# Splitting two casts differently: the first rows of a feed-forward weight cast last, and one low part of a projection weight made by VectorE

## The chip, the core and the metric

One core of a Trainium2 chip runs the whole kernel. The metric is the time of one execution on the device, in microseconds (us). Engines are named as in the profile: PE is TensorE's matmul (PEld its weight load), DVE is VectorE, ACT is ScalarE, POOL is GpSimd, SP is SyncE, which here only issues DMAs.

## What is computed

One transformer-like block on 512 tokens of width 1024, all in float32:

```
parts = split(x @ w_in)                      # att q,k,v; index q,k,w; mlstm q,k,v,i,f,o; two gates
q_a, k_a, q_i, k_i = rope(...)               # cos/sin of position * inv_freq, 32 angles a token
y_a = dsa_attention(q_a, k_a, v, q_i, k_i, w_i)   # index scores, top 128 keys, softmax over those
y_b = sigmoid(o) * head_norm(mlstm(...))
merged = sigmoid(gate_a) * (y_a @ w_up_a) + sigmoid(gate_b) * (y_b @ w_up_b)
h  = layer_norm(alpha * x + merged @ w_out)
ff = square(relu(h @ w_ff1)) @ w_ff2
r  = alpha * h + ff
r  = r + sigmoid(r @ w_ple_gate) * (p @ w_ple_proj)
out = layer_norm(r)
```

## The kernel before, in words

**Products in three parts.** Every float32 matrix is split in a high part (a cast to the type that TensorE multiplies, `hi`) and a low part (`lo = raw - hi`). A product is then three matmuls, `mm3` (L151 to L154): high by high, high by low, low by high. So each weight that arrives by DMA is cast once by ACT and subtracted once, by POOL or DVE, before TensorE can use it. `load_w` (L130) does this for the projections: a DMA on SP's queue into one of three raw buffers, the cast on ACT at L142, the subtraction at L145 in pieces, on POOL unless another engine is given.

**Order.** A scheduler places the instructions of each engine in one fixed order when the kernel is built, from a simulated timeline; `tc.issue_after` makes one instruction stand behind another. At run time each engine works through its own list in that order and waits on semaphores.

**The start.** `take` (L215) loads and splits x. `tables` (L266) issues the steps for the rotation's angles on DVE, each behind the one before; the steps are small (128x128 or 128x256), they end in the tile `rr`, and ACT makes `sind` and `cosd` from it (L276, L278). TensorE first makes the small columns `kv` (L285), then the index queries `iq` with `form_a` (L192): four loads `kk` of 256 rows of weights, two 128-row halves `k` each, for three token tiles. `rope` (L292) then rotates eight pairs of keys `k` of 64 columns (two products from PSUM at L297 and L299 and a sum at L303 whose two inputs are both in SBUF, then a copy on ACT at L305), and after them the tiles of `iq`. The next projection is `aq`, again with `form_a`; its weights are cast at L142 and subtracted on POOL at L145, and its first cast stands on ACT behind the last of the eight key copies.

**Before the feed-forward part.** `ple_projection` (L935) makes eight tiles `ppw` on TensorE, each stored by an ACT copy to `pws` (L943). Among them `h_factors` (L798) turns the last token tiles of h into factors `hc`. The feed-forward product w_ff1 follows a seven-product scheme (P1 to P7, in the order P1, P2, P3, P5, P7, P6, P4 for the first group). `w1_factor` (L911) splits the weight of each product in two halves of 128x1024: rows `0:2` and rows `2:4` of the four 128-row blocks. For P1, P3 and P5 it then adds another quarter of the weight into the raw tile with an accumulating DMA from POOL's queue (L919), which a later product uses: P5's weight is P1's raw tile after that addition. `ff1` (L980) goes through the blocks in the order 0, 1, 2, 3, so its first matmul reads the high part of rows `0:2`.

Of the kernel before, what the change touches and what calls it, by code (L numbers as in the profile page):

```python
# [53 lines left out]
def f(ap):  # L54
    return ap.bitcast(F32)
# [3 lines left out]
def block_kernel(ctx: ExitStack, tc: tile.TileContext, t, out):  # L59
# [67 lines left out]
    def raw_tile(shape, name):  # L127
        return rawpool.tile(shape, F32, tag="wr", bufs=3, name=name)

    def load_w(src, a, b, name, lo_eng=None, off=0, raw=None):  # L130

        raw = raw or raw_tile([P, a, b], name + "r")
        if isinstance(src, list):
            c = 0
            for s_ in src:
                sy.dma_start(raw[:, :, c:c + s_.shape[-1]], s_)
                c += s_.shape[-1]
        else:
            sy.dma_start(raw, src)
        hi, lo = (wpool.tile([P, 1088], F32R, tag="w" + x, bufs=3, name=name + x)[:, off:off + a * b]  # L140
                  .rearrange("p (a b) -> p a b", a=a) for x in "hl")
        se.copy(hi, raw)  # L142
        n = max(1, a // 4)
        for k in range(0, a, n):
            (lo_eng or ge).tensor_sub(lo[:, k:k + n], raw[:, k:k + n], f(hi[:, k:k + n]))  # L145
        return hi, lo

    def chunked(src):
        return src.rearrange("(k p) c -> p k c", p=P)
# [33 lines left out]
    xL = xpool.tile([P, KD, S], F32R, name="xL")  # L183


    def columns(kk, cols, name, lo_eng=None):
        rows = w_in[kk * 256:(kk + 1) * 256]
        return load_w([chunked(rows[:, c0:c0 + n]) for c0, n in cols], 2, sum(c[1] for c in cols), name + "w", lo_eng)

    passed = []  # L190

    def form_a(cols, name, lo_eng=None, first=0, bank=acc):  # L192

        width = sum(c[1] for c in cols)
        banks = {i: (aux if i == 0 else bank)(name + str(i)) for i in range(first, NT)}
        for kk in range(4):
            wh, wl = columns(kk, cols, name, lo_eng)
            for i in banks:
                for k in range(2):
                    kg = kk * 2 + k  # L200
                    mm = mm3(banks[i][:, :width], xH[:, kg, i * P:(i + 1) * P], xL[:, kg, i * P:(i + 1) * P],
                        wh[:, k, :], wl[:, k, :], kg == 0, kg == KD - 1)
            passed.append(mm)
        return banks
# [61 lines left out]
    def tables(n):  # L266

        for _ in range(n):
            with tc.issue_after(vector[-1].ins):
                vector.append(table_steps.pop(0)())  # L270

    for k in range(KD):
        take(k)
        tables({1: 2, 3: 3}.get(k, 0))
    tables(len(table_steps))
    se.activation(sind[:, :, 1, :], sin_, AF.Sin)  # L276
    ve.tensor_scalar(sind[:, :, 0, :], sind[:, :, 1, :], -1.0, None, op0=OP.mult)
    se.activation(cosd[:, :, 0, :], cos_, AF.Sin)  # L278
    ve.tensor_copy(cosd[:, :, 1, :], cosd[:, :, 0, :])
    b1 = [(misc if i else aux)("kv") for i in range(NT)]  # L280
    for k in range(KD):
        wh, wl = (w[:, k % 2] for w in kvw[k // 2][1:])
# [53 lines left out]
    sy.dma_start(cwb, t["conv"])  # L336
    cw, cb = cwb[:, 0:4], cwb[:, 4]

    b3 = form_a([(C_IQ, 512)], "iq", first=1)
    for i in range(NT):  # L340
        ve.tensor_scalar(wi[:, i, :], b1[i][:, 192:200], IDX_W, None, op0=OP.mult)
        ps = misc("kp")
# [499 lines left out]
    def queued(engine, op, *args, **kw):  # L842

        if engine in order_of:
            with tc.issue_after(order_of[engine].ins):
                order_of[engine] = getattr(engine, op)(*args, **kw)  # L846
        else:
            order_of[engine] = getattr(engine, op)(*args, **kw)

    order_of = {}  # L850
# [34 lines left out]
    def w1_rows(t, w):  # L885
        c = groups[t] * 1024 + w[1] * 512
        return w_ff1[w[0] * 512:(w[0] + 1) * 512, c:c + 512].rearrange("(k p) c -> p k c", p=P)

    def w1_load(t, w, issue=None):
# [14 lines left out]
        else:  # L904
            loads.append(sy.dma_start(tl, w1_rows(t, w)))

    W1_OF = {P1: B11, P2: B21, P3: B22, P5: B11, P7: B22, P6: B11, P4: B21}

    W1_ADD = {P1: B12, P5: B22, P3: B12}

    def w1_factor(t, n):  # L911

        tl = w1q[t, W1_OF[n]]
        hi, lo = (pools[1].tile([P, 4, 512], F32R, tag="w1" + x, bufs=2, name="w1" + x) for x in "hl")
        for k in (slice(0, 2), slice(2, 4)):
            queued(se, "copy", hi[:, k], tl[:, k])
            queued(ve, "tensor_sub", lo[:, k], tl[:, k], f(hi[:, k]))
            if n in W1_ADD:
                ge.dma_start(out=tl[:, k], in_=w1_rows(t, W1_ADD[n])[:, k], accum_op=OP.add)  # L919
        if n == P6:  # L920
            for k in (slice(0, 2), slice(2, 4)):
                queued(ve, "tensor_add", w1q[t, B21][:, k], w1q[t, B21][:, k], tl[:, k])
        return hi, lo
# [11 lines left out]
    def ple_projection(i, hh):  # L935

        ps = (aux if (hh, i) == (1, 2) else acc)("ppw")
        tok = slice(i * P, (i + 1) * P)
        projected[:] = [half_product(ps, lambda k: pTH[:, k, tok], lambda k: pTL[:, k, tok], blocks(wp[hh:hh + 1]))]
        if i == 0:  # L940
            pwss.append(gtile("pws", F32))
        pws = pwss[hh][:, i]
        stored[:] = [se.copy(pws, ps)]  # L943
        sy.dma_start(pwd[:, i, hh * 512:(hh + 1) * 512], pws)
# [11 lines left out]
    with tc.issue_after(projected[0].ins):  # L956
        h_factors(NT - 1)
    with tc.issue_after(turned[0].ins):
        for _ in range(2):
            ple_projection(*todo.pop(0))  # L960
    close_ln()
    close_hb()
    pools[0], close_fb = open_pool("fb", side="right")
# [469 lines left out]
```

## Time and profile before

| what | us |
|---|---|
| time before, median of 3 runs | 769.85 (769.58 to 770.32) |
| the profiled execution's own time | 769.99 |
| its span, first to last instruction | 768.3 |
| PE busy / DVE busy / ACT busy / POOL busy | 757.8 / 596.7 / 418.4 / 268.1 |
| TensorE's granted clock, mean over the span | 0.996 |

PE is busy in 99% of the span, so nearly every change of the time has to show as a change of PE's few gaps. All times below are us from the start of the span.

### The profile page before, as it was taken

What the parts mean: (1) busy time and instruction counts of PE and PEld (TensorE: products, weight loads), DVE (VectorE), ACT (ScalarE), POOL (GpSimd) and SP (SyncE); (2) the same over time, 40 slices, a digit from 0 to 9 for tenths busy, and PEclk for the clock granted to TensorE, in tenths of its full rate; (3) what the DMA queues carried; (4) which work ended last, traced back from release to release, by engine and by line L of the source; (5) the groups of instructions that cost most, each with busy time, mean ns of one, the idle gap of its engine ahead of it and who ended that gap; (6) DMA issues with size and microseconds to landing.
All of it is one profiled execution on the core that took longest, in us unless ns stands there. A gap on an engine that the chain in (4) does not pass through costs nothing.

```text
span 768.3 us, 11493 instructions
## 1 busy us (share of the span) xinstructions
PE 757.8 (99%) x4332; PEld 663.2 (86%) x4332; DVE 596.7 (78%) x979; ACT 418.4 (54%) x637; POOL 268.1 (35%) x332
## 2 busy tenths in 40 slices
PE   8999999999999999999999999999999999999995
PEld 8788888889988888878889999999988888888885
DVE  7949999965557987585896767576888988998558
ACT  5546466697756633532366556656565465555210
POOL 6654554444255437470232121212010101126341
PEclk9999999999999999999999999999999999999998
DMA  8443233222223112372089996937497799895202
GB/s 283 127 131 83 56 82 83 83 69 68 71 67 92 62 44 81 91 289 101 1 243 200 335 249 191 238 84 129 112 223 192 144 402 305 140 184 186 93 27 110
DMA packets 77544, 110.43 MB, mean 144 GB/s; under 512 B 3248, under 2 KB 38576, under 8 KB 76208
## 3 DMA queue, kind: packets, MB, share of 16 engines
q1 hardware_dynamic: 58992, 72.76, 28.9%
q0 software_dynamic: 13920, 27.27, 20.6%
q10 hardware_dynamic: 4576, 9.67, 3.6%
q8 instruction: 34, 0.56, 0.3%
q14 instruction: 22, 0.18, 0.1%
HBM read 101.29 MB, written 8.39 MB: 143 GB/s over the span
## 4 chain that ended last, share of the span: by engine, by line
PE 94%; DVE 3%; issue 1%; POOL 1%; DMA 1%; DVEq 0%; ACT 0%; POOLq 0%
PE pf L993 21%; PE pf L1224 20%; PE pg L152 5%; PE pg L154 5%; PE pg L153 5%; PE pu L154 2%; PE pu L152 2%; PE pu L153 2%; PE po L152 2%; PE po L154 2%; PE po L153 2%; PE ptp L480 1%; PE kv L285 1%; PE mv L154 1%; PE mv L153 1%
## 5 line engine op out<-in xcount | busy, mean ns | idle before, releaser
L846 DVE TENSOR_TENSOR w1l<-w1q,w1h 128x1024 fp32r<-128x1024 f32 x55 | 65.0, 1222 | 34.8 <-ACT w1h L846 34.4
L846 DVE TENSOR_TENSOR wl<-b,wh 128x2048 fp32r<-128x2048 f32 x28 | 64.8, 2313 | 10.4 <-ACT wh L846 10.4
L846 ACT CAST w1h<-w1q 128x1024 fp32r<-128x1024 f32 x55 | 55.3, 1048 | 23.6 <-PE pf L993 20.6
L919 POOL DMA_DIRECT2D w1q<-in_w_ff x24 | 29.2, 1254 | 111.7 <-DVE w1l L846 108.4
L145 POOL TENSOR_TENSOR wgl<-wgr,wgh 128x256 fp32r<-128x256 f32 x64 | 49.9, 813 | 47.5 <-ACT wgh L142 47.5
L1074 POOL DMA_DIRECT2D b<-in_w_ff x14 | 17.9, 1279 | 133.3 <-DVE wl L846 125.6
L1224 PE MATMUL pf<-wh,ah 128*128 128x512 f32 x216 | 58.1, 391 | 0.0
L1224 PE MATMUL pf<-wh,al 128*128 128x512 f32 x216 | 57.8, 389 | 0.0
L846 ACT CAST wh<-b 128x2048 fp32r<-128x2048 f32 x28 | 53.5, 1909 | 3.2 <-DMA b<-in_w_ff 3.2
L1224 PE MATMUL pf<-wl,ah 128*128 128x512 f32 x216 | 53.5, 390 | 0.0
L154 PE MATMUL pg<-xH,wgl 128*128 128x512 f32 x128 | 50.6, 395 | 0.0
L152 PE MATMUL pg<-xH,wgh 128*128 128x512 f32 x128 | 50.4, 394 | 0.0
L153 PE MATMUL pg<-xL,wgh 128*128 128x512 f32 x128 | 50.3, 393 | 0.0
L1224 PEld LDWEIGHTS pf<-wh,al 128*128 128x128 f32 x216 | 40.6, 188 | 8.5
L1224 PEld LDWEIGHTS pf<-wh,ah 128*128 128x128 f32 x216 | 40.3, 188 | 8.7 <-ACT wh L846 0.4
L1224 PEld LDWEIGHTS pf<-wl,ah 128*128 128x128 f32 x216 | 40.5, 188 | 8.4
L145 POOL TENSOR_TENSOR wul<-wur,wuh 128x128 fp32r<-128x128 f32 x64 | 36.6, 605 | 19.0 <-ACT wuh L142 19.0
L846 DVE TENSOR_TENSOR c<-c,pf 128x512 f32<-128x512 f32 x48 | 30.5, 683 | 10.2 <-ACT c L846 10.2
L846 ACT ACTIVATE c<-c 128x1024 f32<-128x1024 f32 x12 | 12.7, 1061 | 31.3 <-DVE c L846 31.3
L767 POOL TENSOR_TENSOR lag<-lag,mhalf 128x1 f32<-128x1 f32 x8 | 7.5, 941 | 61.1 <-DVE lag L766 61.1
L153 PEld LDWEIGHTS pg<-xL,wgh 128*128 128x128 f32 x128 | 24.1, 188 | 4.6
L152 PEld LDWEIGHTS pg<-xH,wgh 128*128 128x128 f32 x128 | 24.1, 188 | 4.5
(396 smaller groups left out, 2297.1 us busy)
## 6 DMA issues: line engine op xcount, KB each, us to landing
b<-in_w_ff POOLq DMA_DIRECT2D x14, 1024.0 KB, 9.1
w1q<-in_w_ff POOLq DMA_DIRECT2D x24, 512.0 KB, 7.6
w1q<-in_w_ff SPq DMA_DIRECT2D x9, 1024.0 KB, 7.6
wgr<-in_w_in SPq DMA_DIRECT2D x16, 512.0 KB, 3.8
b<-in_w_ff SPq DMA_DIRECT2D x8, 1024.0 KB, 7.0
wor<-in_w_out SPq DMA_DIRECT2D x8, 512.0 KB, 7.3
b<-in_w_ff ACTq DMA_DIRECT2D x4, 1024.0 KB, 8.8
wpgr<-in_w_ple_gate SPq DMA_DIRECT2D x8, 512.0 KB, 9.1
```

Source lines behind the costliest of these rows:

```text
L145: (lo_eng or ge).tensor_sub(lo[:, k:k + n], raw[:, k:k + n], f(hi[:, k:k + n]))
L152: te.matmul(ps, sh, mh, start=first, stop=False, **kw)
L153: te.matmul(ps, sh, ml, start=False, stop=False, **kw)
L154: return te.matmul(ps, sl, mh, start=False, stop=last, **kw)
L285: te.matmul(b1[i][:, :208], (xH, xL, xH)[kind][:, k, i * P:(i + 1) * P], (wh, wh, wl)[kind], start=k == 0 and kind == 0, stop=k == KD - 1 ...
L480: te.transpose(ps[:, slot * P:(slot + 1) * P], prs[slot // 2][:, slot % 2, j * P:(j + 1) * P], ident)
L767: ge.tensor_tensor(out=ag[:, 3:4], in0=ag[:, 2:3], in1=mhalf[:, 0:1], op=OP.pow))
L846: order_of[engine] = getattr(engine, op)(*args, **kw)
L919: ge.dma_start(out=tl[:, k], in_=w1_rows(t, W1_ADD[n])[:, k], accum_op=OP.add)
L993: mm = te.matmul(ps, w[:, k, b * P:(b + 1) * P], a[:, k], start=fresh, stop=w is lo and k == 3, skip_group_check=True)
L1074: return ge.dma_start(out=tl, in_=rows_of(g, w), accum_op=OP.add)
L1224: mm = te.matmul(banks[n, s], (al if kind == 1 else ah)[:, q, tok], (wl if kind == 2 else wh)[:, q], start=fresh and kind == 0 and q == 0, ...
```

## The change

Two edits, without new arithmetic.

First, `form_a` for `iq` gives the list of DVE's table steps as `low_by`. For the first load (`kk` 0) the low part of its first half (`k` 0, 128x512) is then made by DVE and put in the chain behind the table step that was last issued; the rest of the low parts stays on POOL. So that there are steps left to stand behind, `tables` is called for two steps only ahead of the `kv` matmuls, and for the rest, with the two sine activations and the two copies, after `form_a`.

Second, `w1_factor` for the first product (group 0, P1) splits rows `2:4` first and leaves rows `0:2` to a function `finish`, which is called in the last two tiles of `ple_projection`: the cast of rows `0:2` stands behind the store of the seventh tile `ppw`, and its subtraction and its accumulating DMA behind that.

```
-    def load_w(src, a, b, name, lo_eng=None, off=0, raw=None):
+    def load_w(src, a, b, name, lo_eng=None, off=0, raw=None, first=None):
...
         for k in range(0, a, n):
-            (lo_eng or ge).tensor_sub(lo[:, k:k + n], raw[:, k:k + n], f(hi[:, k:k + n]))
+            if k == 0 and first:
+                with tc.issue_after(first[-1].ins):
+                    first.append(ve.tensor_sub(lo[:, k:k + n], raw[:, k:k + n], f(hi[:, k:k + n])))
+            else:
+                (lo_eng or ge).tensor_sub(lo[:, k:k + n], raw[:, k:k + n], f(hi[:, k:k + n]))
...
-            wh, wl = columns(kk, cols, name, lo_eng)
+            wh, wl = columns(kk, cols, name, lo_eng, None if kk else low_by)
...
-    tables(len(table_steps))
-    se.activation(sind[:, :, 1, :], sin_, AF.Sin)
-    ve.tensor_scalar(sind[:, :, 0, :], sind[:, :, 1, :], -1.0, None, op0=OP.mult)
-    se.activation(cosd[:, :, 0, :], cos_, AF.Sin)
-    ve.tensor_copy(cosd[:, :, 1, :], cosd[:, :, 0, :])
+    tables(2)
...
-    b3 = form_a([(C_IQ, 512)], "iq", first=1)
+    b3 = form_a([(C_IQ, 512)], "iq", first=1, low_by=vector)
+    tables(len(table_steps))
+    se.activation(sind[:, :, 1, :], sin_, AF.Sin)
+    ve.tensor_scalar(sind[:, :, 0, :], sind[:, :, 1, :], -1.0, None, op0=OP.mult)
+    se.activation(cosd[:, :, 0, :], cos_, AF.Sin)
+    ve.tensor_copy(cosd[:, :, 1, :], cosd[:, :, 0, :])
...
-        for k in (slice(0, 2), slice(2, 4)):
+        def part(k):
             queued(se, "copy", hi[:, k], tl[:, k])
             queued(ve, "tensor_sub", lo[:, k], tl[:, k], f(hi[:, k]))
+
+        def add(k):
             if n in W1_ADD:
                 ge.dma_start(out=tl[:, k], in_=w1_rows(t, W1_ADD[n])[:, k], accum_op=OP.add)
+
+        if t == 0 and n == P1:
+
+            part(slice(2, 4))
+            add(slice(2, 4))
+
+            def finish(wait):
+                with tc.issue_after(wait.ins):
+                    order_of[se] = se.copy(hi[:, 0:2], tl[:, 0:2])
+                queued(ve, "tensor_sub", lo[:, 0:2], tl[:, 0:2], f(hi[:, 0:2]))
+                add(slice(0, 2))
+
+            late.append(finish)
+        else:
+            for k in (slice(0, 2), slice(2, 4)):
+                part(k)
+                add(k)
...
     with tc.issue_after(turned[0].ins):
-        for _ in range(2):
-            ple_projection(*todo.pop(0))
+        ple_projection(*todo.pop(0))
+        late.pop()(stored[0])
+        ple_projection(*todo.pop(0))
```

How this moves the engines' lists at three places. On DVE, among the table steps (`rr`, `kq` and `ang` are their tiles; `iqwl` is the low part of the index queries' weights, `wi` small columns taken from the `kv` banks). Before:

```order
L256 SCALAR_TENSOR_TENSOR rr<-kq,rr 128x256
L257 SCALAR_TENSOR_TENSOR rr<-kq,rr 128x256
L258 TENSOR_SCALAR rr<-rr 128x128
L259 TENSOR_SCALAR kq<-rr 128x256
L260 TENSOR_TENSOR rr<-rr,kq 128x256
L261 TENSOR_SCALAR kq<-rr 128x256
L262 TENSOR_TENSOR rr<-rr,kq 128x256
L263 TENSOR_SCALAR rr<-rr 128x256
L341 TENSOR_SCALAR wi<-kv 128x8
L277 TENSOR_SCALAR sind<-sind 128x4x32
L279 COPY cosd<-cosd 128x4x32
L341 TENSOR_SCALAR wi<-kv 128x8 x3
```

The same place on DVE in the changed kernel:

```order
L260 SCALAR_TENSOR_TENSOR rr<-kq,rr 128x256
L147 TENSOR_TENSOR iqwl<-iqwr,iqwh 128x512
L261 SCALAR_TENSOR_TENSOR rr<-kq,rr 128x256
L262 TENSOR_SCALAR rr<-rr 128x128
L263 TENSOR_SCALAR kq<-rr 128x256
L264 TENSOR_TENSOR rr<-rr,kq 128x256
L265 TENSOR_SCALAR kq<-rr 128x256
L266 TENSOR_TENSOR rr<-rr,kq 128x256
L267 TENSOR_SCALAR rr<-rr 128x256
L346 TENSOR_SCALAR wi<-kv 128x8 x4
L342 TENSOR_SCALAR sind<-sind 128x4x32
L344 COPY cosd<-cosd 128x4x32
```

One subtraction stands new between the second and the third of the last steps (seven of them follow it), and all four `wi` stand ahead of the copies of the sines. POOL's list has seven subtractions `iqwl` in place of eight.

On ACT, among the key copies, where the cast of the fourth load of index weights `iqwh` stands (the numbers tell the eight keys `k` apart). Before:

```order
L305 COPY k_418<-k_418 128x64
L114 CAST vHL<-kv 128x64
L305 COPY k_426<-k_426 128x64
L351 CAST vH_302<-kv 128x64
L305 COPY k_443<-k_443 128x64
L142 CAST iqwh<-iqwr 128x1024
L114 CAST vHL<-kv 128x64
```

The same place in the changed kernel:

```order
L305 COPY k_418<-k_418 128x64
L114 CAST vHL<-kv 128x64
L305 COPY k_426<-k_426 128x64
L356 CAST vH_291<-kv 128x64
L142 CAST iqwh<-iqwr 128x1024
L305 COPY k_443<-k_443 128x64
L114 CAST vHL<-kv 128x64
```

The fourth cast stands one key copy earlier. TensorE's order inside `iq` changes a little with this (it takes the low part sooner), and nothing behind `iq` does.

On ACT ahead of the first feed-forward product (`w1h` is the high part of a w_ff1 weight, `pws` the stored `ppw` tiles, `hb`, `a` and `hc` tiles of `h_factors`). Before:

```order
L848 CAST w1h<-w1q 128x1024
L846 CAST w1h<-w1q 128x1024 x3
L810 COPY hb_3977<-hps_4326 128x4x128
L114 CAST hc1H<-hps_4326 128x4x128
L943 COPY pws<-ppw 128x512 x2
L814 COPY a_4419<-hps_4410 128x512
L114 CAST hc2H<-hps_4410 128x4x128
L943 COPY pws<-ppw 128x512 x2
L114 CAST hc3H<-hps_4410 128x4x128
```

The same place in the changed kernel:

```order
L853 CAST w1h<-w1q 128x1024
L815 COPY hb_3977<-hps_4326 128x4x128
L114 CAST hc1H<-hps_4326 128x4x128
L969 COPY pws<-ppw 128x512 x2
L819 COPY a_4416<-hps_4407 128x512
L114 CAST hc2H<-hps_4407 128x4x128
L969 COPY pws<-ppw 128x512
L937 CAST w1h<-w1q 128x1024
L851 CAST w1h<-w1q 128x1024 x2
L969 COPY pws<-ppw 128x512
L114 CAST hc3H<-hps_4407 128x4x128
```

The first cast is now that of rows `2:4` of P1; rows `0:2` (L937) stand behind the seventh store, and the two casts of P2 (L851 x2) behind that. TensorE's order from `ppw` into the first product `pf` is the same in both.

## Rows read from the trace of the kernel before

**Rows 1.** The page, first part: busy time of PE and the other engines, share of the span, instructions.

```profile
PE 757.8 (99%) x4332; PEld 663.2 (86%) x4332; DVE 596.7 (78%) x979; ACT 418.4 (54%) x637; POOL 268.1 (35%) x332
```

**Rows 2.** The waits of PE over the whole span: who it waited for, us in total, times, longest.

```profile
PE iq L153 <- POOL iqwl L145: 0.3, 1, 0.3
```

**Rows 3.** The timeline of PE at the fourth load of `iq`: start, duration, engine, line, operation, out and in.

```profile
29.68 0.39 PE L152 MATMUL iq<-iqwh,xH 128*128 128x512 f32 x1
30.14 0.50 PE L153 MATMUL iq<-iqwl,xH 128*128 128x512 f32 x1
30.48 0.39 PE L154 MATMUL iq<-iqwh,xL 128*128 128x512 f32 x1
...
31.38 0.50 PE L153 MATMUL iq<-iqwl,xH 128*128 128x512 f32 x1 [0.27 <-POOL iqwl L145]
31.72 0.39 PE L154 MATMUL iq<-iqwh,xL 128*128 128x512 f32 x1
```

**Rows 4.** The timeline of PE in `aq`, at the first matmuls that read the second and the fourth low part.

```profile
36.49 0.43 PE L153 MATMUL aq<-aqwl,xH 128*128 128x512 f32 x1
...
39.05 0.39 PE L152 MATMUL aq<-aqwh,xH 128*128 128x512 f32 x1
39.38 0.50 PE L153 MATMUL aq<-aqwl,xH 128*128 128x512 f32 x1
```

**Rows 5.** The timeline of POOL: the first, seventh and eighth low part of `iq`, then the first four of `aq` in two rows of two.

```profile
16.16 1.49 POOL L145 TENSOR_TENSOR iqwl<-iqwr,iqwh 128x512 fp32r<-128x512 f32 x1 [2.06 <-ACT iqwh L142]
...
28.80 1.29 POOL L145 TENSOR_TENSOR iqwl<-iqwr,iqwh 128x512 fp32r<-128x512 f32 x1 [4.43 <-ACT iqwh L142]
30.05 1.28 POOL L145 TENSOR_TENSOR iqwl<-iqwr,iqwh 128x512 fp32r<-128x512 f32 x1
33.37 3.00 POOL L145 TENSOR_TENSOR aqwl<-aqwr,aqwh 128x512 fp32r<-128x512 f32 x2 [2.05 <-ACT aqwh L142]
36.33 3.00 POOL L145 TENSOR_TENSOR aqwl<-aqwr,aqwh 128x512 fp32r<-128x512 f32 x2
```

**Rows 6.** The timeline of DVE: a 128x512 subtraction while POOL is idle, the table steps (the first of the last seven as POOL begins), and three of the `wi` columns.

```profile
4.98 0.69 DVE L226 TENSOR_TENSOR xL<-xrs,xH 128x512 fp32r<-128x512 f32 x1 [3.75 <-ACT xH L224]
...
11.36 0.29 DVE L254 TENSOR_SCALAR kq<-kq 128x256 f32<-128x256 f32 x1
...
16.08 0.43 DVE L257 SCALAR_TENSOR_TENSOR rr<-kq,rr 128x256 f32<-128x256 f32 x1
16.54 1.20 DVE L258 TENSOR_SCALAR rr<-rr 128x128 f32<-128x128 f32 x1
...
19.10 1.40 DVE L260 TENSOR_TENSOR rr<-rr,kq 128x256 f32<-128x256 f32 x1
...
23.26 1.26 DVE L263 TENSOR_SCALAR rr<-rr 128x256 f32<-128x256 f32 x1
...
25.25 0.30 DVE L341 TENSOR_SCALAR wi<-kv 128x8 f32<-128x8 f32 x3
```

**Rows 7.** The timeline of DVE: the fifth, sixth and seventh key sum, and the first step of the rotation of `iq`.

```profile
28.57 0.23 DVE L303 TENSOR_TENSOR k<-t,t 128x64 f32<-128x64 f32 x1
...
29.38 0.79 DVE L303 TENSOR_TENSOR k<-t,t 128x64 f32<-128x64 f32 x1
...
30.61 0.81 DVE L303 TENSOR_TENSOR k<-t,t 128x64 f32<-128x64 f32 x1
...
32.23 0.68 DVE L297 TENSOR_TENSOR t<-iq,cosd 128x512 f32<-128x512 f32 x1
```

**Rows 8.** The timeline of ACT: the first cast of index weights, then the places around the fourth and around the first of `aq`.

```profile
15.03 1.05 ACT L142 CAST iqwh<-iqwr 128x1024 fp32r<-128x1024 f32 x1 [0.88 <-DMA iqwr<-in_w_in]
...
27.00 0.21 ACT L351 CAST vH<-kv 128x64 fp32r<-128x64 f32 x1
27.53 0.24 ACT L305 COPY k<-k 128x64 f32<-128x64 f32 x1 [0.31 <-DVE k L303]
27.68 1.05 ACT L142 CAST iqwh<-iqwr 128x1024 fp32r<-128x1024 f32 x1
...
32.25 1.05 ACT L142 CAST aqwh<-aqwr 128x1024 fp32r<-128x1024 f32 x1
```

**Rows 9.** The timeline of ACT: the fourth store of a `ppw` tile and the first cast for P1; then the first casts for P5.

```profile
394.60 0.58 ACT L943 COPY pws<-ppw 128x512 f32<-128x512 f32 x1 [0.80 <-PE ppw L154]
395.09 1.05 ACT L848 CAST w1h<-w1q 128x1024 fp32r<-128x1024 f32 x1
...
410.88 2.00 ACT L846 CAST w1h<-w1q 128x1024 fp32r<-128x1024 f32 x2 [1.18 <-PE pf L993]
```

**Rows 10.** The timeline of PE: the last matmul of the seventh `ppw` tile, the last of the eighth, and the first of the feed-forward product.

```profile
399.65 0.40 PE L154 MATMUL ppw<-wp,pT 128*128 128x512 f32 x1
...
401.03 0.39 PE L154 MATMUL ppw<-wp,pT 128*128 128x512 f32 x1
401.25 0.64 PE L993 MATMUL pf<-hc0H,w1h 128*128 128x256 f32 x4
```

**Rows 11.** The raw tiles of w_ff1 from 380 to 425 us: time from a DMA's issue to its landing.

```profile
DMA to landing us min/median/max: 5.4/7.7/10.5
```

**Rows 12.** Busy time by stretch, the feed-forward part from 420 to 480 us: length, then PE, PEld, DVE, ACT and POOL busy with instructions, clock, DMA share, GB/s.

```profile
420.00:480.00 60.00, 60.00 (x512) 60.00 (x511) 43.32 (x47) 34.92 (x43) 9.65 (x8) 1.00 0.91 257
```

**Rows 13.** The page's costliest groups: the subtraction of a w_ff1 half on DVE (us in all, mean ns of one, idle time before).

```profile
L846 DVE TENSOR_TENSOR w1l<-w1q,w1h 128x1024 fp32r<-128x1024 f32 x55 | 65.0, 1222 | 34.8 <-ACT w1h L846 34.4
```

More of the change, by code (lines that the diff above doesn't have):

```diff
@@ L183, in block_kernel, with columns, form_a @@
     xL = xpool.tile([P, KD, S], F32R, name="xL")
-    def columns(kk, cols, name, lo_eng=None):
+    def columns(kk, cols, name, lo_eng=None, first=None):
         rows = w_in[kk * 256:(kk + 1) * 256]
-        return load_w([chunked(rows[:, c0:c0 + n]) for c0, n in cols], 2, sum(c[1] for c in cols), name + "w", lo_eng)
+        return load_w([chunked(rows[:, c0:c0 + n]) for c0, n in cols], 2, sum(c[1] for c in cols), name + "w", lo_eng, first=first)
     passed = []
-    def form_a(cols, name, lo_eng=None, first=0, bank=acc):
+    def form_a(cols, name, lo_eng=None, first=0, bank=acc, low_by=None):
         width = sum(c[1] for c in cols)
@@ L905, in w1_load @@
             loads.append(sy.dma_start(tl, w1_rows(t, w)))
+    late = []
     W1_OF = {P1: B11, P2: B21, P3: B22, P5: B11, P7: B22, P6: B11, P4: B21}
```

## The prediction

> **What bounds the kernel now.** I read the page's busy times first: PE is busy in 757.8 of 768.3 us [rows 1], so the time can only move where PE stands still or where something makes it stand still. The waits of PE come next: behind the first 10 us the only entry is 0.3 us in `iq`, for a low part from POOL [rows 2]. That entry understates the loss, because a late operand also shows as matmuls that start further apart than the 0.23 us of their neighbours. So I read PE's starts. From 29.68 to 31.72 us there are five steps, which at 0.227 us would take 1.13 us and take 2.04: 0.9 us are lost at the fourth load of `iq`, where the two low parts end on POOL at 30.09 and 31.33 and the matmuls that read them start at 30.14 and 31.38 [rows 3, 5]. A little further, in `aq`, the second and the fourth low part end at 36.37 and 39.33 and are read at 36.49 and 39.38 [rows 4, 5]: PE loses only about 0.1 us there, but both arrive just in time, with no slack. Around the second edit PE has nothing to win: the eighth `ppw` tile runs straight into the feed-forward product [rows 10], and the feed-forward part is full, 60.00 us busy in a window of 60.00 [rows 12].
>
> **First edit: one low part from POOL to DVE.** It removes one POOL subtraction and adds one on DVE. These two engines do not run such work side by side. The step L258 begins at 16.54 and lasts 1.20 us, ending 0.09 us after POOL's first subtraction ends at 17.65; a like step takes 0.29 us with POOL idle; L260 and L263 last 1.40 and 1.26 us [rows 5, 6]. From 17.65 to the end of L263 at 24.52 are five more POOL subtractions, each with a table step behind it, so a pair costs 6.87 / 5 = 1.37 us.
>
> In the changed kernel ACT's first cast ends at 16.08 [rows 8]. I let DVE go first: its subtraction takes 0.69 us with POOL idle [rows 6] and ends at 16.80. POOL's own half of that load then ends at about 18.08 (1.28 us, [rows 5]). Four more pairs follow to 23.56, the step L261 ends 0.15 us later, and the last two steps run free, 0.43 and 0.29 us [rows 6]: the tables end at 24.45 instead of 24.52. One POOL operation fewer pays for one DVE operation more, and for no more than that.
>
> Which engine goes first is not in the trace. Rows are near: POOL starts 0.08 us after the cast that it waits for [rows 5, 8], and at 16.08 the table step L257 was already running and took its undisturbed 0.43 us while POOL, issued at 16.16, needed 1.49 instead of 1.28. So the one that is first holds the other up, and DVE, which is free at that moment, is likely first. The Trainium skill says the same of the mechanism and speaks against this edit (SBUF, State Buffer, section "Who interferes with whom"): a VectorE instruction with two SBUF inputs contends with a GpSimd instruction that reads SBUF, and whoever issues first blocks the other in full. The rows above agree (1.20 us for a step of 0.29). By that rule the work moved is not work made parallel, which is my sum above; were the two side by side, the tables would end near the time of their own steps, some 5 us sooner, and the first rival below would be the likeliest.
>
> What follows the tables: three `wi` columns (0.30 us [rows 6]) now run while ACT makes the sines; I take 0.1 us of gain from that, so the keys start 0.17 us earlier. The fourth cast stands one key copy earlier on ACT, right behind the copy at 27.00 and not behind the one at 27.53 [rows 8]: it starts near 27.0 instead of 27.68, and POOL's last two `iqwl` end near 29.40 and 30.70 instead of 30.09 and 31.33. PE wants them at 29.91 and 30.59. So the 0.9 us at the fourth load go, or nearly.
>
> But they are not won. The key sums L303 have two SBUF inputs, 0.23 us alone and 0.79 and 0.81 us beside POOL [rows 7]. Before, the sixth and the seventh met POOL's two subtractions. With POOL earlier, the fifth (near 28.40, held until 29.47) and the sixth (near 30.05, held until 30.8) meet them, and the seventh runs free 0.44 us later and ends near 31.47 instead of 31.42. The rotation of `iq` then starts at 32.28 instead of 32.23, the cast for `aq` behind the last key copy at 32.30 instead of 32.25, and the `aqwl` chain on POOL, which starts when that cast is done, is 0.05 us later too. PE arrives 0.9 us sooner at `aq` and waits there for the second low part until 36.42 instead of 36.37. **First edit: +0.05 us.** Bounds: from -0.2 (the sines' gain is 0.3) to +0.35 (POOL first, below), and -0.9 if `aq` does not hold PE up at all.
>
> **Second edit: rows 0:2 of P1 cast last.** Nothing is added; a cast, a subtraction and an accumulating DMA move back. Behind the seventh `ppw` tile, which ends at 399.65 + 0.40 = 400.05 [rows 10], ACT stores it and only then makes that cast. The start-to-start time of the same pair is 0.49 us, the cast takes 1.05 [rows 9]: 400.07 + 0.49 + 1.05 = 401.61. PE needs this half for its very first feed-forward matmul, which stood at 401.25 [rows 10]; between 400.05 and there it has only the eighth tile. With a weight load ahead of it, that matmul starts at about 401.70, 0.45 us late, and the next may follow late too, as the matmul after a held one does (0.34 against 0.23 us, [rows 3]). I take **+0.5 us**, from 0.35 to 0.65. This does not depend on where the first edit leaves PE, since both ends of the race start at the seventh tile. What moves forward for it, two `h_factors` copies, is for P2, 5.6 us later, and was in time; the feed-forward part has no gap for it to close [rows 12]. P2's casts end near 403.6 and the eighth store near 404.1, both ahead of 406.9, when P2 begins.
>
> **Sum.** The profiled execution took 769.99 us; +0.05 and +0.5 give 770.54. That execution lies 0.14 above the median of the runs, so in those terms **770.4 us**. About 0.2%, 1.54 us, is what a measurement of this kernel can tell from no change.
>
> **The rivals.**
> *The 0.9 us are won.* For it: they are there in PE's starts. Against it: the two just-in-time parts of `aq`, which start from an ACT cast behind the last key. It needs the key chain to come 0.8 us sooner. -0.9 + 0.5: 769.45 us.
> *POOL goes first at 16.1.* DVE's subtraction then ends near 18.05; PE, which wants it at 17.62, waits 0.45 us, and that is hidden by its later wait; but the tables end some 0.25 us later and the `aq` chain with them: +0.3 + 0.5, 770.65 us.
> *The late cast costs nothing* (PE is held behind the seventh tile for another reason, or ACT comes through sooner): 769.9 us. I see no row for it.
> *Slower by over 0.2%: the moved accumulating DMA.* Rows 0:2 of P1's raw tile get their addition only after the moved subtraction (1.22 us [rows 13], behind four steps of `h_factors` on DVE: issued near 403.5, not 397.9). P5's cast reads them; before it started at 410.88 [rows 9]. Landing takes 5.4 to 10.5 us, 7.7 at the median [rows 11]: 411.2, at worst 414.0. PE wants P5 three products after P1; 48 matmuls of 60.00 / 512 us are 5.63 each [rows 12], so at 418.6 with the half microsecond, and the first half must land by 417.5. From 14 us on each microsecond of landing costs one, and at 15 us the kernel would be at 771.4. No landing in the rows is near it.
>
> **How the numbers follow.** The forecast (+0.2 to +0.9) 0.60; the 0.9 us won, in full or for the larger part, 0.17; POOL first 0.10; the late cast free 0.08; the late DMA 0.03; something unseen 0.02. The range 769.4 to 771.1 takes in the sum's own bounds (-0.2 + 0.35 to +0.35 + 0.65 on 769.85, so 770.0 to 770.85), the first and the third rival, and 0.25 us above for the scatter of the runs shown. All cases but the DMA's lie within 1.54 us of 769.85, so: faster by over 0.2% 0.03, within 0.2% 0.90, slower 0.07 (the DMA and the sums of several bounds).
>
> **What would show it.** Right: PE's steps at the fourth load of `iq` even, 0.23 us apart; a stop of 0.6 to 0.9 us in front of the `aq` matmul that reads the second low part; `rr` done within 0.15 us of 24.5; the cast for `aq` within 0.3 us of 32.25; on PE a stop of about half a microsecond ahead of the first `pf` matmul, released by ACT's L937, and none behind it. Wrong: PE early by 0.5 us or more behind `aq`, DVE and POOL overlapping among the tables, no stop at the first `pf`, or a stop at P5 released by a DMA.

## The result: two kinds of times, and a profile of each

| | median, us | all executions, us | ratio to before |
|---|---|---|---|
| before | 769.91 | 769.31 to 770.56 (20) | 1 |
| changed | 764.67 | 763.60 to 765.42 (15) and 769.91 to 771.01 (5) | 0.9949, interval 0.9936 to 0.9961 |

The forecast was 770.4 us, within 0.2% of the kernel before; the changed kernel is 0.5% faster, and its median lies below the forecast range. One thing is needed to understand the number: the same program has two kinds of executions, some 5.5 us apart, at the same granted clock (0.996 to 0.998), and the profile that came with the result is one of the long kind (770.02 us). A second profile, of a short execution (764.25 us), was taken later; it is the one called short below (label after_again).

The long kind first, because it answers the steps of the prediction. Its busy line, then PE's waits (who it waited for: us in total, times, longest):

```profile
PE 758.0 (99%) x4332; PEld 663.5 (86%) x4332; DVE 595.8 (78%) x980; ACT 419.0 (55%) x637; POOL 268.2 (35%) x331
```

```profile
PE aq L157 <- POOL aqwl L149: 0.4, 1, 0.4
PE pf L1020 <- ACT w1h L937: 0.3, 1, 0.3
```

Against [rows 1, 2] the busy times stand where they stood; the wait in `iq` has gone, one in `aq` and one at the first `pf` have come. Two pieces of PE's timeline of this execution, at the fourth `iq` load and in `aq` (start, duration, engine, line, operation):

```profile
29.80 0.39 PE L157 MATMUL iq<-iqwl,xH 128*128 128x512 f32 x1
30.03 0.39 PE L158 MATMUL iq<-iqwh,xL 128*128 128x512 f32 x1
30.25 0.39 PE L156 MATMUL iq<-iqwh,xH 128*128 128x512 f32 x1
...
35.30 0.39 PE L156 MATMUL aq<-aqwh,xH 128*128 128x512 f32 x1
36.11 0.50 PE L157 MATMUL aq<-aqwl,xH 128*128 128x512 f32 x1 [0.42 <-POOL aqwl L149]
```

The steps at the fourth load, uneven in [rows 3], are now 0.22 to 0.27 us; instead PE stands 0.81 us between two matmuls of `aq`, and the second low part is read at 36.11, where [rows 4] had 36.49.

Then the place of the second edit. PE in the long execution, in the short one, and in the kernel before (the rows behind those of [rows 10]):

```profile
400.77 0.39 PE L158 MATMUL ppw<-wp,pT 128*128 128x512 f32 x1
401.41 0.74 PE L1020 MATMUL pf<-hc0H,w1h 128*128 128x256 f32 x4 [0.25 <-ACT w1h L937]
401.98 0.64 PE L1020 MATMUL pf<-hc0L,w1h 128*128 128x256 f32 x4
402.45 0.64 PE L1020 MATMUL pf<-hc0H,w1h 128*128 128x256 f32 x4
```

```profile
400.81 0.39 PE L158 MATMUL ppw<-wp,pT 128*128 128x512 f32 x1
401.45 0.72 PE L1020 MATMUL pf<-hc0H,w1h 128*128 128x256 f32 x4 [0.25 <-ACT w1h L937]
402.01 0.62 PE L1020 MATMUL pf<-hc0L,w1h 128*128 128x256 f32 x4
402.46 0.62 PE L1020 MATMUL pf<-hc0H,w1h 128*128 128x256 f32 x4
```

```profile
401.73 0.64 PE L993 MATMUL pf<-hc0L,w1h 128*128 128x256 f32 x4
402.20 0.63 PE L993 MATMUL pf<-hc0H,w1h 128*128 128x256 f32 x4
402.67 0.63 PE L993 MATMUL pf<-hc0L,w1h 128*128 128x256 f32 x4
```

The stop is the same in both executions of the changed kernel: the first `pf` matmul starts 0.64 us behind the last `ppw` matmul. What differs comes after it. Groups of four 256-column matmuls start 0.47 us apart in the long execution and in the kernel before, and 0.45 in the short one. The starts one by one give 117.8 ns from matmul to matmul before and in the long execution, 113.3 ns in the short one, nearly without scatter (117 to 119, and 113 to 114). There are 1344 of these matmuls between 401 and 563 us: 1344 x 4.44 ns = 5.97 us. The window of [rows 12], in the long and then in the short execution (length, PE busy with its instructions, granted clock, DMA share, GB/s):

```profile
420.00:480.00 60.00, 60.00 (x512) 1.00 0.93 260
```

```profile
420.00:480.00 60.00, 60.00 (x532) 1.00 0.96 269
```

PE is busy for 60.00 of 60.00 us in both, at a granted clock of 1.00, and does 20 matmuls more in one of them. From the last `ppw` matmul to the last 256-column `pf` the kernel before takes 162.13 us and the short execution 156.69: 0.52 us lost at the stop, 5.97 won behind it. The spans differ by 768.3 - 762.5 = 5.8 us.

The weight loads tell the two spacings apart as well. Sixteen of them in the kernel before, in the short execution, and in a run that comes later (stops_a); the three figures are the shortest, the median and the longest in ns:

```profile
L993 PEld LDWEIGHTS pf<-hc5H,w1l x16: 187/188/192, 427.5 to 429.3; 128*128 128x128 f32 x16
L1020 PEld LDWEIGHTS pf<-hc5H,w1l x16: 187/188/188, 426.8 to 428.5; 128*128 128x128 f32 x16
L993 PEld LDWEIGHTS pf<-hc5H,w1l x16: 192/192/192, 433.0 to 434.8; 128*128 128x128 f32 x16
```

From 420 to 480 us one load in three lasts 192 ns in the kernel before (169 of 509), and none of 530 in the short execution. That the longer loads make the wider spacing is not shown; the two go together in every trace of this case.

### The profile page after: what moved, and what is told of

Its sections match the earlier page's. It is cut to its first block, busy times and chain, and to the rows that moved or that the text cites. A ratio compares the mean times of both kernels' runs of the same rounds, so it can differ in the third digit from the quotient of the medians.

```text
span 768.3 us, 11493 instructions
## 1 busy us (share of the span) xinstructions
PE 758.0 (99%) x4332; PEld 663.5 (86%) x4332; DVE 595.8 (78%) x980; ACT 419.0 (55%) x637; POOL 268.2 (35%) x331
## 4 chain that ended last, share of the span: by engine, by line
PE 92%; DVE 3%; DMA 2%; POOL 1%; issue 1%; ACT 0%; DVEq 0%; SPq 0%; POOLq 0%
PE pf L1020 21%; PE pf L1251 20%; PE pg L156 5%; PE pg L158 5%; PE pg L157 5%; PE pu L158 2%; PE pu L156 2%; PE pu L157 2%; PE po L158 2%; PE po L157 2%; PE po L156 2%; DMA xrs<-in_xt 1%; PE ptp L485 1%; POOL iqwl L149 1%; PE mv L158 1%
## 5 line engine op out<-in xcount | busy, mean ns | idle before, releaser
L851 DVE TENSOR_TENSOR w1l<-w1q,w1h 128x1024 fp32r<-128x1024 f32 x55 | 64.9, 1222 | 34.2 <-ACT w1h L851 31.6
L851 DVE TENSOR_TENSOR wl<-b,wh 128x2048 fp32r<-128x2048 f32 x28 | 64.8, 2314 | 11.0 <-ACT wh L851 11.0
L851 ACT CAST w1h<-w1q 128x1024 fp32r<-128x1024 f32 x54 | 54.4, 1051 | 24.5 <-PE pf L1020 21.7
L851 ACT CAST wh<-b 128x2048 fp32r<-128x2048 f32 x28 | 53.5, 1911 | 4.9 <-DMA b<-in_w_ff 4.9
L851 DVE TENSOR_TENSOR c<-c,pf 128x512 f32<-128x512 f32 x48 | 30.5, 683 | 10.2 <-ACT c L851 10.2
L851 ACT ACTIVATE c<-c 128x1024 f32<-128x1024 f32 x12 | 12.7, 1062 | 31.3 <-DVE c L851 31.3
```

## The experiments

"Short" and "long" are executions at 763.6 to 765.5 us and at 769.1 to 771.1; the close spacing is 113.3 ns from start to start, the long one 117.8. The kernel before was run beside all of them and never went under 769.1 us. Spacings are read from PE's starts in the trace of the execution that was profiled.

**Each edit alone, and the changed kernel again.** Labels e1_only, e2_only, after_again; the first keeps only the part of the diff around `form_a` and `tables`, the second only that around `w1_factor`.

> The first edit alone (low part on VectorE, tables interleaved), the cast order of w1 as before. The changed kernel has two kinds of times, 763.6 to 765.4 us in 15 of 20 runs and 769.9 to 771.0 in 5, the kernel before only 769.3 to 770.6. Theory A (the short kind comes from the start, whatever happens at the first pf): this kernel has times near 764.2 us in most runs. Theory B (the short kind needs the stop of 0.3 us ahead of the first pf matmul): all runs at 769.3 to 769.9, the 0.3 us won behind aq and nothing else. Theory C (both edits needed): as B here, and as before in the other one.

> The second edit alone (rows 0:2 of P1 cast last), the start as before. Theory A: all runs at 770.2 to 770.6 us, half a microsecond above the kernel before. Theory B (the stop ahead of the first pf matmul decides): times near 764.5 us in most runs, with the rest near 770.4. Theory C (both edits needed): as A.

> The changed kernel once more, to have a trace of its short kind: three chances in four that this execution takes 763.6 to 765.4 us. If the 5.5 us are one stop that goes, they are in one stretch and the windows show it; if they are a closer spacing of the matmuls, they are spread over hundreds of matmuls of one form, with the busy share of PE unchanged.

Measured: the first edit alone 769.94 us, 11 of 11 long, ratio 0.9998 (0.9990 to 1.0007). The second alone 764.89 us, 5 of 6 short, 0.9943 (0.9925 to 0.9961). The changed kernel again: short, the trace shown above, with 1342 of the 1344 steps at 113 or 114 ns. Theory B stands and A and C fall: the second edit brings it alone. The profiled execution of the second edit is its one long one (769.86 us), and shows why it is long. PE by stretches of 20 us (columns as above):

```profile
420.00:440.00 20.00, 20.00 (x179) 1.00 0.97 303
440.00:460.00 20.00, 19.70 (x170) 1.00 1.09 285
460.00:480.00 20.00, 20.00 (x173) 1.00 0.75 206
```

and what lies between the first and the third row, in PE's timeline:

```profile
446.34 0.71 PE L1015 MATMUL pf<-hc6H,w1h 128*128 128x256 f32 x4 [0.30 <-DVE c L846]
446.88 0.63 PE L1015 MATMUL pf<-hc6L,w1h 128*128 128x256 f32 x4
```

It had the 113.3 ns for 43 us, over one uneven step of 136 ns at 429.7, then PE waited once for VectorE, and behind that stop it had 117.8 up to 557.8 us. So a stop can end the close spacing as well as begin it, and a spacing held here until something disturbed PE.

**A bare stop in the same place.** Label stop_only, on the kernel before:

```diff
         ple_projection(*todo.pop(0))
+        with tc.issue_after(stored[0].ins):
+            order_of[se] = se.copy(w1[0][:, 0:2], f(w1[0][:, 0:2]))
         ple_projection(*todo.pop(0))
```

> The kernel before with one operation more: behind the seventh ppw store ACT copies rows 0:2 of P1's high part onto themselves, 1.05 us, so that PE's first pf matmul waits for ACT as in the changed kernel (it starts about 0.64 us behind the one ahead of it, where before it was 0.23), while the cast, the subtraction and the accumulating DMA stay where they were. The trace of the short kind has the 256-column matmuls of the first feed-forward product 113.3 ns apart, the long kind and the kernel before 117.8, 1344 of them: 6.0 us. Theory D (the stop lets PE begin in the close spacing, whatever makes the stop): about three runs in four at 764.6 us, the others at 770.4. Theory E (the moved cast, subtraction or DMA changes what runs beside PE, and that sets the spacing): all runs at 770.4.

Measured: 770.07 us, 2 of 12 short (764.05, 764.37), ratio 0.9987 (0.997 to 1.0005). The two short ones say that no moved cast, subtraction or DMA is needed, against theory E; but the share of 2 in 12 is far from the three in four of theory D. Its profile (a long execution) has the same stop, 401.04 to 401.68:

```profile
401.04 0.39 PE L154 MATMUL ppw<-wp,pT 128*128 128x512 f32 x1
401.68 0.74 PE L995 MATMUL pf<-hc0H,w1h 128*128 128x256 f32 x4 [0.25 <-ACT w1h L961]
402.25 0.64 PE L995 MATMUL pf<-hc0L,w1h 128*128 128x256 f32 x4
```

Neither theory holds as it was put.

**Matmuls of another width, without any stop.** Label probe, on the kernel before, in `ff1`:

```diff
+                    if n not in (P6, P4) and kinds[0][0] is hi and b == 0:
+                        q = WIDTHS.pop(0)
+                        te.matmul(ps[:, 0:q], hi[:, 0, 0:P], ah[:, 0, 0:q], start=True, stop=False, skip_group_check=True)
```

> The kernel before with a matmul more ahead of 20 of the 28 products of the first feed-forward part, of a width of 64, 128, 192, 224, 240, 32, 160, 96, 208 or 248 columns, each width twice; what it writes is overwritten by the product's first matmul, so it is work added. Some 110 ns each: 2.2 us by itself, 772.1 us if the spacing stays at 117.8 ns throughout. Theory F (the spacing is a phase between weight loads and matmuls that holds itself, and a matmul of another width can shift it): at some of the 20 places the spacing changes from 117.8 to 113.3 ns or back and then holds up to the next place; the same width does the same from the same state. Theory G (only a real stop changes it): 117.8 at all of them.

Measured: 769.61 us, with ten changes of the spacing at the 20 places, each holding up to the next inserted matmul or the next stretch of another width. Two neighbouring places as PE's timeline shows them, 32 columns at 440.64 and 96 at 452.17:

```profile
440.64 0.18 PE L992 MATMUL pf<-hc0H,w1h 128*128 128x32 f32 x1
440.67 0.72 PE L997 MATMUL pf<-hc0H,w1h 128*128 128x256 f32 x4
441.22 0.63 PE L997 MATMUL pf<-hc0L,w1h 128*128 128x256 f32 x4
...
452.17 0.21 PE L992 MATMUL pf<-hc1H,w1h 128*128 128x96 f32 x1
452.21 0.70 PE L997 MATMUL pf<-hc1H,w1h 128*128 128x256 f32 x4
452.75 0.62 PE L997 MATMUL pf<-hc1L,w1h 128*128 128x256 f32 x4
453.20 0.62 PE L997 MATMUL pf<-hc1H,w1h 128*128 128x256 f32 x4
```

Behind the 32 columns the groups of four are 0.47 us apart, behind the 96 columns 0.45. Nothing waits at either place. G falls, and F's forecast came: a single matmul of another width, without a stop, can change the spacing, and the new one then holds. That a phase between weight loads and matmuls is what holds itself is F's picture of it; no view shows that phase. The first inserted matmul, 64 columns ahead of the first `pf`, changed the entry from the long to the close spacing.

**That one matmul alone.** Labels dummy64 (on the kernel before) and e1_dummy64 (on the first edit alone): the same insertion with `WIDTHS = [64]` and nothing else.

> The kernel before with one matmul of 64 columns more, directly ahead of the first pf matmul (what it writes is overwritten by that matmul); no stop, no cast moved. In the trace with a matmul ahead of 20 products this one brought the spacing from 117.8 to 113.3 ns (30 and 199 ns for it and its successor instead of 118: 0.11 us). Theory F (the spacing is a phase that holds itself, and only how PE enters the stretch counts): 770.0 - 1344 x 4.44 ns + 0.11 = 764.1 us in all or nearly all runs, and no second kind of times. Theory I (the phase is lost or found by chance on the way, as with the stops): two kinds again, 764.1 and 770.1, with some share.

> The first edit with the 64-column matmul ahead of the first pf matmul, and no second edit. Theory F: 764.0 us in all or nearly all runs, below the median of the changed kernel (764.7) and without its long kind; the first edit adds -0.3 to 0 to it. Theory I: two kinds, as in the other kernel with this matmul.

Measured: dummy64 763.93 us (763.71 to 764.93), 5 of 5 short, ratio 0.9926 (0.9914 to 0.9939); e1_dummy64 764.56 us (764.06 to 764.63), 5 of 5 short, 0.9932 (0.9918 to 0.9945). PE's timeline in dummy64, and its window of 60 us:

```profile
400.88 0.39 PE L154 MATMUL ppw<-wp,pT 128*128 128x512 f32 x1
401.11 0.19 PE L993 MATMUL pf<-hc0H,w1h 128*128 128x64 f32 x1
401.14 0.71 PE L998 MATMUL pf<-hc0H,w1h 128*128 128x256 f32 x4
401.68 0.62 PE L998 MATMUL pf<-hc0L,w1h 128*128 128x256 f32 x4
```

```profile
420.00:480.00 60.00, 60.00 (x532) 1.00 0.94 265
```

No stop, no cast moved, 113.3 ns from the start on. Work added makes the kernel 5.9 us faster, by what the sum said: 5.97 - 0.11. It is the shortest version here, and none of the ten executions with this matmul was long: theory F's forecast of 764.1, not theory I's two kinds. The first edit adds nothing that these runs can show.

**The changed kernel with its gain taken away.** Label after_dummy32: the changed kernel with `WIDTHS = [0, 32]`, that is, one matmul of 32 columns ahead of the second product.

> The changed kernel with one matmul of 32 columns more, ahead of the second product of the first feed-forward part (P2), overwritten like the others. In the trace with 20 such matmuls one of 32 columns led from 113.3 to 117.8 ns and left 117.8 as it was. Theory F: the stop ahead of the first pf matmul, the moved cast and its DMA are all still there, and the gain is gone: 769.9 to 770.6 us in all runs. If the moved cast, subtraction or DMA were the cause of the shorter time: 764 to 765 us in about three runs of four.

Measured: 770.30 us, 10 of 10 long (769.33 to 770.83), ratio 1.0004 (0.9995 to 1.0013). The profile shows both spacings, on either side of the 32 columns at 406.48:

```profile
401.94 0.62 PE L1025 MATMUL pf<-hc0H,w1h 128*128 128x256 f32 x4
402.40 0.62 PE L1025 MATMUL pf<-hc0L,w1h 128*128 128x256 f32 x4
...
406.48 0.18 PE L1020 MATMUL pf<-hc1H,w1h 128*128 128x32 f32 x1
406.50 0.72 PE L1025 MATMUL pf<-hc1H,w1h 128*128 128x256 f32 x4
407.06 0.64 PE L1025 MATMUL pf<-hc1L,w1h 128*128 128x256 f32 x4
407.53 0.64 PE L1025 MATMUL pf<-hc1H,w1h 128*128 128x256 f32 x4
```

All of the edit is still there, the stop too, and the gain is gone, as theory F said. So the gain is the spacing, and not the moved cast, subtraction or DMA.

**Does the width settle the spacing?** Label probe2, other widths at the 20 places.

> As the trace with 20 matmuls, with other widths: 64, 96, 32, 208, 32, 64, 32, 96, 64, 32, 112, 112, 32, 80, 80, 32, 128, 128, 64, 64. It asks whether the spacing after a matmul of a given width follows from that width and the spacing ahead of it. If it does: 32 leads to 117.8 ns from both, 96 from 117.8 to 113.3, 128 changes either into the other. If it is chance, the same width from the same spacing gives both.

Measured: 770.77 us. Both traces together, by the spacing ahead of the inserted matmul:

| from | to 113.3 ns | to 117.8 ns |
|---|---|---|
| the last `ppw` | 64 (twice) | |
| 113.3 ns | 192, 208 (twice), 224 | 32, 64 (three times), 80, 96, 128, 240, 248 (twice) |
| 117.8 ns | 32 (once), 80, 96 (three times), 128 (twice), 240 | 32 (six times), 64 (twice), 112 (twice), 128 (once), 160 (twice), 192, 208, 224 |

From the close spacing each width that was tried more than once gave one result. From the long one 32 and 128 gave both, so "32 leads to 117.8 from both" was wrong once in eight, and the width alone does not settle it there. The steps of the long spacing are not all alike (117, 118, 119 in turns), so the matmul can meet them at more than one point; that this is the reason was not tested.

**Many stops in one execution.** Labels stops_a and stops_b, on the kernel before, ahead of 27 products:

```diff
+        if k:
+            queued(se, "copy", scr, w1_banks(*last)[1][:, 496:512])
+            queued(se, "copy", w1[0][:, 0, 0:128], f(w1[0][:, 0, 0:128]))
```

> The kernel before with a stop ahead of 27 of the 28 products of the first feed-forward part: ACT copies 16 columns of the product just ended, and then 128 columns of the next high part onto themselves, and the product's first matmul waits for that. Work added, about 0.5 us a stop: 780 to 786 us. It asks whether a stop settles the spacing. Theory J (the phase in which PE is released decides, and one stop is as good as a throw): behind some stops 113.3 ns, behind others 117.8, in one execution, each holding up to the next stop. Theory K (what the stop waits for decides): the same spacing behind all of them.

> The same with 512 columns copied onto themselves, so that each stop is some 0.3 to 0.4 us longer: 790 to 797 us. Theory J: again both spacings, with another share. Theory K: one spacing behind all, perhaps not that of the shorter stops.

Measured: 798.95 and 808.0 us, each stop longer than I had taken (0.74 to 1.25 us from start to start in the first, 1.06 to 1.57 in the second). PE's waits in stops_a:

```profile
PE pf L993 <- ACT w1h L846: 17.4, 25, 1.0
```

Behind these stops the spacing was neither of the two, but 120 ns, and it was so ahead of the first stop (at 408.4 us) too:

```profile
403.22 0.64 PE L993 MATMUL pf<-hc0L,w1h 128*128 128x256 f32 x4
403.70 0.64 PE L993 MATMUL pf<-hc0H,w1h 128*128 128x256 f32 x4
404.18 0.64 PE L993 MATMUL pf<-hc0L,w1h 128*128 128x256 f32 x4
```

The groups of four stand 0.48 us apart, where the kernel before has 0.47, and nearly every weight load lasts 192 ns. Already from 341 us on, in the 512-column matmuls of the product ahead of `ppw`, the usual step is 233 ns where it is 227 in all other runs. Something else than the stops differs in these two programs; their edit also adds a tile, `scr`, of 16 columns, and whether that is the reason was not tested. So the two runs do not decide between J and K: one spacing behind all the stops is what K said, but here neither 113.3 nor 117.8 came up at any of them.

**What in the stop decides.** Labels e2_again (the second edit alone once more), stop_later and stop_sooner (the bare stop with 1246 and 802 columns copied instead of 1024), and e2_no_add:

```diff
                 queued(ve, "tensor_sub", lo[:, 0:2], tl[:, 0:2], f(hi[:, 0:2]))
-                add(slice(0, 2))
```

> The second edit alone once more, on the same chip as the next three, to know its share of short executions there (5 of 6 before, and 16 of 21 with both edits). If the share is a matter of the chip, it differs here as it does for the bare stop; if it belongs to the edit, it is again near three in four, 764.9 us, the others near 770.

> The bare stop, with 1246 columns copied onto themselves where it was 1024: PE is released about 0.19 us later, at the same point of VectorE's work on the h factors as with the moved cast (its step from PSUM then begins 0.36 us ahead of the first pf matmul, where the bare stop had 0.17). Theory L (what runs beside the first matmuls after the release decides): the share of short executions goes from 2 in 12 to about three in four. Theory M (the moved DMA decides): it stays near 2 in 12. Theory J (the fine phase of the release): any share.

> The bare stop with 802 columns copied onto themselves, PE released about 0.19 us sooner than with 1024. Theory L: no more short executions than with 1024, 2 in 12. Theory M: the same. Theory J: any share, another one than with 1246 columns.

> The second edit with the accumulating DMA of rows 0:2 of P1's raw tile left out (the sum that P5 needs is then wrong in these rows). Theory M (the accumulating DMA, which runs at another moment than before, decides): the share of short executions falls to 2 in 12 or none. Theories L and J: it stays near three in four.

Measured: e2_again 764.63 us, 8 of 11 short, so 13 of 17 in all; stop_later 764.79 us and stop_sooner 764.55 us, 5 of 5 short each, ratios 0.9930 (0.9919 to 0.9942) and 0.9927 (0.9915 to 0.9939); e2_no_add 766.41 us, 6 of 12 short, 5 long and one at 767.40, the profiled one. In that one PE entered in the close spacing and was then disturbed four times: the close spacing came back behind the steps of 529 and 558 ns at 429.5 and 446.1 us, the long one came behind a step of 417 ns at 468.6, and the close one again behind two uneven steps (146 and 193 ns) at 485.8. PE's first `pf` matmuls in stop_later:

```profile
401.81 0.74 PE L996 MATMUL pf<-hc0H,w1h 128*128 128x256 f32 x4 [0.44 <-ACT w1h L962]
402.39 0.62 PE L996 MATMUL pf<-hc0L,w1h 128*128 128x256 f32 x4
```

The share of the second edit did not change with the chip: 5 of 6 on one, 8 of 11 on another. The bare stop of 1024 columns ran on one chip only, and not on that of these four runs, so for its 2 in 12 the chip is not excluded. Theory L fits stop_later and falls with stop_sooner, where VectorE stands at another point and all five are short. Theory M wanted 2 in 12 or none without the added DMA; 6 in 12 lies between that and three in four and decides nothing, but the bare stops without any moved DMA refute the DMA as a need. What remains of J: the disturbances in the one profiled execution of e2_no_add led into either spacing, and a bare stop released 0.19 us sooner or later than that of 2 in 12 gave 5 of 5, twice (with the chip as said).

Open stays why the moved cast and the bare copy of the same length differ (13 of 17 against 2 of 12). The traces have a hint: of the seven profiled executions with this stop, three entered in the long spacing, and in all three the first `pf` matmul started 640 ns behind the last `ppw` matmul (after, stop_only, e2_again); in the four that entered in the close one it started 638, 639, 641 and 641 ns behind it (e2_no_add, after_again, e2_only, after_dummy32). That fits a moment of release that counts to the nanosecond; seven executions do not show it.

## Why the prediction was wrong, point by point

**The step that failed** is the sentence on the second edit, "the feed-forward part has no gap for it to close [rows 12]", and with it the opening claims that PE is full there and has nothing to win, and that the time can only move where PE stands still. The row says 60.00 of 60.00, and I read a full busy share as full speed. In the same row stand 512 matmuls in 60.00 us, 0.117 us for 256 columns; for 512 columns my sum on `iq` took 0.227 us. I used both numbers and did not put one beside the other: half of 227 ns is 113.5, not 118. That difference of some 4 ns, 1344 times, is what came: 113.3 ns a matmul instead of 117.8, 5.97 us that the sum put at nothing. No row of before tells that this edit would change it. The Trainium skill (Perfetto Trace Analysis, section "Identifying the Most-Contended Engine") says that TensorE's matmul busy share is not a good measure of the distance to the best it can do, and names the busy share of weight loads beside the flops achieved instead; the trace agrees with the first (x512 and x532 at the same 60.00), and of the second only the count of matmuls tells the two executions apart, since the weight loads' row is full as well in [rows 12].

**The second edit's own cost** was right: the first `pf` matmul 0.42 us later behind the eighth tile (0.45 forecast), released by ACT, the next one 0.10 us late, +0.52 against +0.5. The term that was missing is -5.97 us behind it, in three executions of four.

**The first edit** was mis-sized: +0.05 forecast, about -0.25 found. The last `ppw` matmul starts at 401.06 us in the median of ten profiles without this edit (400.88 to 401.55) and at 400.81 in that of the five with it (400.27 to 400.97); stops_a and stops_b, with their 233 ns steps on the way, are left out. The two ranges overlap, and the whole times of e1_only do not show so little. DVE did go first, as I took it to (its timeline, at the low part and the table step behind it):

```profile
15.99 0.69 DVE L147 TENSOR_TENSOR iqwl<-iqwr,iqwh 128x512 fp32r<-128x512 f32 x1 [0.15 <-ACT iqwh L142]
16.60 1.51 DVE L261 SCALAR_TENSOR_TENSOR rr<-kq,rr 128x256 f32<-128x256 f32 x1
```

and the steps behind it stood beside POOL at 1.2 to 1.5 us each, as in [rows 6]. (The step by which the prediction shows the two engines' blocking, L258, has one input in SBUF; a step with two is L260, 1.40 us in [rows 6].) The tables ended at 24.18 us, not 24.45; 0.13 of the difference is an earlier first cast (14.90, against [rows 8]), the rest is mine. The fifth and sixth key sums met POOL, as I said (1.06 and 0.82 us), but the cast for `aq` came at 31.94, not 32.30, and the second low part was read at 36.11, not 36.42. `aq` did hold PE up, so the 0.9 us of the fourth load, which the first rival took as won, were not won in full; what was found lies between that rival and the forecast, 0.05 us outside my bounds for this term.

**The sum without the new spacing** was nearly right: the long executions have a median of 770.02 us, 0.1 above the kernel before, where -0.25 + 0.52 give +0.27 and the last 47 matmuls of the profiled one, at 113.3 ns behind a switch of width, give 0.2 back.

**The rivals.** POOL did not go first. The late cast was not free. The late DMA came, and cost nothing. In the profiled long execution P5's cast started at 411.13, released by PE, against 410.88 in [rows 9]; in four other profiles with the second edit it was the DMA that released this cast, at 412.05 to 413.51, inside the 411.2 to 414.0 that the prediction gave, and PE waited nowhere from 410 to 425 us. The short execution's cast:

```profile
412.05 1.05 ACT L851 CAST w1h<-w1q 128x1024 fp32r<-128x1024 f32 x1 [3.45 <-DMA w1q<-in_w_ff]
```

That the time would end on the fast side by over 0.2% had 0.03; the case that came had no mechanism in the text, only the 0.02 for something unseen. The list of what would make the prediction wrong had four items, and none was a spacing that changes without a wait.

## What to carry to other kernels

For an engine that is busy all the time, compare the time per column (or per element) of its forms with each other: where one runs at 0.460 ns per column (256 columns in 117.8 ns) and another at 0.443 (512 in 227) on the same type, the difference times the count may be a reserve, though no wait shows it. If the starts of a long uniform stretch are even but wider than that, try what lies at its entry, a matmul of another width or a few tenths of a microsecond; it may cost one line. And when a change wins much more than its parts can, look for its two kinds of executions before explaining it, and take the gain away from the changed kernel as well as giving it to the old one.

## What the runs showed of the hardware that I had not expected

- A stream of pairs of a 128x128 weight load and a 256-column matmul had two steady spacings in this kernel, 113.3 and 117.8 ns, at a granted clock of 1.00 in both, and a third, 120 ns, in the two programs with many stops. The loads last 187 or 188 ns in the first, one in three lasts 192 in the second, nearly all do in the third. The first held for up to 147 us in one piece, the second for up to 152, and both were left only where PE's steps had been disturbed: at a stop or an uneven step, at a matmul of another width, or behind a stretch of 512 columns. The Trainium skill (TensorE: Matmul & The Clock Gate, section "Back-to-back issue gap") says that the spacing in such a stream is set by load and matmul together; nothing here speaks against it, but the same pair showed three values.
- A 64-column matmul more ahead of the stretch made the kernel 5.9 us shorter (769.83 to 763.93 us); a 32-column matmul more took 5.6 us away from the changed kernel (764.67 to 770.30).
- A stop of 0.64 us ahead of the stretch led into either spacing, in shares of 13 of 17 and 2 of 12 by how it was made; bare stops 0.19 us shorter or longer led into the close one in 10 of 10 executions, on another chip than the bare stop of 0.64.
